# Two PSUM copies per scan step moved from VectorE to ScalarE in a two-layer hybrid trunk

## The chip, the cores and the metric

One core of one Trainium2 chip runs the whole program. The metric is device time in microseconds (us), the median over the runs of the kernel. TensorE is PE in the rows, VectorE DVE, ScalarE ACT, GpSimd POOL, SyncE SP; PEld is TensorE's loading of weights.

## The reference

Two layers, each with three parallel mixers over 128 context tokens and 512 latent tokens, D_MODEL 1024. Mixer C is a bidirectional scan with a delta rule; it is the part that the change touches:

```python
def step(state, inp):
    r_t, w_t, k_t, v_t, a_t, b_t = inp
    sa = jnp.einsum('bhij,bhj->bhi', state, a_t)
    state = (state * w_t[:, :, None, :] + sa[..., None] * b_t[:, :, None, :]
             + v_t[..., None] * k_t[:, :, None, :])
    y_t = jnp.einsum('bhij,bhj->bhi', state, r_t)
    return state, y_t
...
for d, s0 in ((0, s0_f), (1, s0_b)):
    ...
    s_fin, y_d = _wkv_scan(s0.astype(f32), rh, hd(decay), k_d, vh, -kk, kk * hd(a), reverse=(d == 1))
```

Everything else (attention of mixers A and B, gates, projections, norms) stays as it is.

## The kernel before

The program is written tile by tile; a scheduler with its own model of times then puts the instructions of each engine into one fixed order, and each engine runs its list in that order. So an instruction that waits holds back all that stands behind it on its engine. When a line moves to another engine, the scheduler makes the whole order anew.

The tokens of mixer C are cut into ten chunks of 64 (two of context, eight of latent tokens), the eight heads into four pairs. For a pair of heads `prepare` does in turn `c_prep` (decays, keys), `c_pairs` (products inside a chunk, tiles `L1` and `AB`), `c_inverse` and `c_bonus`; then `c_scan` walks the ten chunks, both directions and both heads at once. While the scan of pair p runs, the code draws from a stream (`pump`): the preparation of pair p+1, and projections of 128 columns (tile `pcm`, lines 227 to 229, "fillers" below) whose weights (two buffers) are loaded, rounded on ScalarE (`whi`, line 176) and subtracted on VectorE or GpSimd (`wlo`, line 177).

`c_inverse` (lines 653 to 702) inverts the triangular blocks. Its core is one chain on VectorE: a transpose (line 656), 30 steps of a product (line 662, writes `NF`) and a sum (line 664, writes `LN`), a transpose (line 666), two copies (line 673, with two of ScalarE at line 671) and a last transpose (line 674). Then TensorE has two rounds of small 32x32 products, `px` (line 683) and `py` (line 695), with copies between them. There are eight such inversions, four in each layer.

A scan step, of which a scan has ten and the program 80, goes like this:
- line 771: eight products into PSUM tile `sca` from the state half and the value half of `VZ`;
- lines 773 and 774: the first 64 rows of `sca`, one copy for each head, into `Wb` (tile `wbd`), 64x128 elements each;
- line 777: products of `Wb` with `AB` (the inverse) into `scb`;
- lines 779 and 780: `scb`, one copy for each head, into `VZ`;
- line 782: GpSimd copies that into `Ub` (`ubd`); line 786: products for the state from `VZ`; line 790: products from `Ub`, added in `sca`;
- line 803: VectorE updates the state in `VZ` with four instructions; line 808: ScalarE copies the outputs from `sca` into `YY`.

`Wb` and `Ub` have two buffers each, `VZ` one. After the scan `c_gn` normalises (lines 818 to 834, mostly VectorE) and `c_out` transposes and adds (`pyt`, lines 847 to 852) inside the next scan. The last scan of a layer has hardly any projections beside it for its first steps.

Of the kernel before, what the change touches and what calls it, by code (L numbers as in the profile page):

```python
# [107 lines left out]
class Trunk:  # L108
# [595 lines left out]
    def c_scan(self, l, e, ps, rate, prev):  # L704

        nc, V, S, G, PE = self.nc, self.V, self.S, self.G, self.PE
        sm = cs = self.cs
        p, L1, AB, BT, gm, VZ = e.p, e.L1, e.AB, e.BK, e.gm, e.VZ

        def pc(name):  # L710
            return ps.tile([128, 512], F32, tag="c", name=name)

        PR = (slice(0, 64), slice(64, 128))
        QR = (slice(64, 128), slice(0, 64))

        e.YY = YY = cs.tile([128, 20, 64], F32, tag="YY", name="YY")
        step = 0
        for n, base in ((2, 0), (8, 2)):
            ctxp = n == 2
            if ctxp:  # L720
                for h in range(2):
                    G.memset(VZ[h][PR[h], 0:2, :], 0.0)
                Zg = sm.tile([128, 2, 64], F32, tag="Zg", name="Zg", bufs=2)
                G.memset(Zg, 0.0)
            else:
                Z0 = sm.tile([128, 2, 64], F32, tag="Z0", name="Z0")
                nc.sync.dma_start(out=Z0, in_=self.I["zinit"][l, p])
                for h in range(2):
                    r_ = PR[h]
                    S.copy(out=VZ[h][r_, base, :], in_=Z0[r_, 0])  # L730
                    S.mul(out=VZ[h][r_, base + n - 1, :], in_=Z0[r_, 1], mul=gm[r_, 10 + base + n - 1:10 + base + n])

            def pair(cf, cb):

                a, b = base + cf, base + cb
                if a < b:
                    return slice(a, b + 1, b - a)
                return slice(a, b - 1 if b else None, b - a)

            for k in range(n):  # L740
                cf, cb = k, n - 1 - k
                up = pair(cf, cb)
                uu = (base + cf, 10 + base + cb)
                cc = (base + cf, base + cb)
                last = k == n - 1
                need_z = ctxp or not last
                gi = (base + k, None if last else 10 + base + n - 2 - k)
                if need_z and not (ctxp and k == 0):
                    Zg = sm.tile([128, 2, 64], F32, tag="Zg", name="Zg", bufs=2)
                    for h in range(2):  # L750
                        r_ = PR[h]
                        if not last:
                            g2 = gm[r_, gi[0]:gi[1] + 1:gi[1] - gi[0]]
                            G.tensor_tensor(out=Zg[r_], in0=VZ[h][r_, up, :], in1=g2.unsqueeze(2).to_broadcast([64, 2, 64]),
                                            op=ALU.mult)
                        else:
                            G.tensor_scalar(out=Zg[r_, 0], in0=VZ[h][r_, cc[0], :], scalar1=gm[r_, gi[0]:gi[0] + 1],
                                            scalar2=None, op0=ALU.mult)
                            G.tensor_copy(out=Zg[r_, 1], in_=VZ[h][r_, cc[1], :])
                Wb, Ub = self.wbd[step % 2], self.ubd[step % 2]  # L760
                step += 1
                if step == 5 and prev:
                    self.c_out(prev, ps)
                ca, cb_ = pc("sca"), pc("scb")

                a4 = ca[:, 0:256].rearrange("p (d h i) -> p d h i", d=2, h=2)
                b4 = cb_.rearrange("p (x d h i) -> p x d h i", x=2, d=2, h=2)

                for h in range(2):
                    for d in range(2):  # L770
                        PE.matmul(a4[:, d, h], lhsT=L1[h][:, uu[d]].rearrange("p a s -> p (a s)"), rhs=VZ[h][:, cc[d], :],  # L771
                                  start=(h == 0 and d == 0), stop=False, skip_group_check=True)
                S.copy(out=Wb[PR[0], :, 0], in_=a4[0:64, :, 0])
                V.tensor_copy(out=Wb[PR[1], :, 1], in_=a4[0:64, :, 1])
                self.pump(rate)
                for d in range(2):
                    PE.matmul(cb_[:, d * 128:d * 128 + 128], lhsT=AB[:, uu[d]].rearrange("p a s -> p (a s)"),
                              rhs=Wb[:, d].rearrange("p h i -> p (h i)"), start=True, stop=True, skip_group_check=True)
                S.copy(out=VZ[0][PR[0], up, :], in_=b4[0:64, 0, :, 0])  # L779
                V.tensor_copy(out=VZ[1][PR[1], up, :], in_=b4[0:64, 0, :, 1])  # L780
                for h in range(2):
                    G.tensor_copy(out=Ub[PR[h], :, h], in_=VZ[h][PR[h], up, :])  # L782
                self.pump(rate)
                if need_z:
                    for d in range(2):
                        PE.matmul(cb_[:, 256 + d * 128:384 + d * 128], lhsT=BT[:, uu[d]].rearrange("p h i -> p (h i)"),  # L786
                                  rhs=e.VZt[:, :, cc[d], :], start=True, stop=True, skip_group_check=True)
                self.pump(rate)
                for d in range(2):
                    PE.matmul(ca[:, d * 128:d * 128 + 128], lhsT=AB[:, uu[d]].rearrange("p a s -> p (a s)"),  # L790
                              rhs=Ub[:, d].rearrange("p h i -> p (h i)"), start=False, stop=True, skip_group_check=True)
                if need_z:
                    if last:
                        Zf = sm.tile([128, 2, 64], F32, tag="Zf", name="Zf")
                    for h in range(2):
                        r_ = PR[h]
                        for d in range(2):
                            src = b4[r_, 1, d, h]
                            dst = Zf[r_, d] if last else VZ[h][r_, cc[d] + (1 if d == 0 else -1), :]
                            if gi[d] is None:  # L800
                                V.tensor_tensor(out=dst, in0=src, in1=Zg[r_, d], op=ALU.add)
                            else:
                                V.scalar_tensor_tensor(out=dst, in0=src, scalar=gm[r_, gi[d]:gi[d] + 1], in1=Zg[r_, d],  # L803
                                                       op0=ALU.mult, op1=ALU.add)
                    if last:
                        nc.sync.dma_start(out=self.O["nst"][l, p], in_=Zf)
                for h in range(2):
                    S.copy(out=YY[QR[h], uu[0]:uu[1] + 1:uu[1] - uu[0], :], in_=a4[64:128, :, h])
# [833 lines left out]
```

## Time and profile before

| what | value |
|---|---|
| median of 3 runs | 2282.05 us (2279.15 to 2290.32) |
| the profiled execution | 2288.99 us |
| its span, first to last instruction | 2287.3 us |
| mean granted TensorE clock | 0.947 of 2.4 GHz |
| TensorE busy | 2112.1 us (92%) |
| VectorE busy | 1547.8 us (68%) |
| ScalarE busy | 1155.0 us (50%) |
| GpSimd busy | 528.7 us (23%) |

A row of waits names who waited, for whom, how long in total, how often, and the longest. A clock of 1.00 in a stretch is 2.4 GHz, 0.50 is 1.2 GHz. The scans run from about 114 us to 740 us (layer 0) and from about 1310 us to 1832 us (layer 1).

### The profile page before, as it was taken

How to read it: one execution, taken by the hardware profiler on the slowest of the kernel's cores; microseconds unless marked ns; L12 is line 12 of the kernel's file. 1: busy time of each engine (PE TensorE's matmuls, PEld its weight loads, DVE VectorE, ACT ScalarE, POOL GpSimd, SP SyncE). 2: the span in 40 equal slices, each digit the busy share in tenths (PEclk: the TensorE clock that was granted, in tenths of full speed). 3: DMA queues.
4: the chain of work that ended last, by engine and by line, in shares of the span. 5: the costliest groups of instructions: out<-in, count | busy, mean ns of one | idle time of the engine just before them, and what ended most of it. 6: DMA issues, size and time to landing. Idle time of an engine off the chain costs nothing.

```text
span 2287.3 us, 40446 instructions
## 1 busy us (share of the span) xinstructions
PE 2112.1 (92%) x15380; PEld 2004.8 (88%) x15380; DVE 1547.8 (68%) x3096; ACT 1155.0 (50%) x2574; POOL 528.7 (23%) x680
## 2 busy tenths in 40 slices
PE   8989999999889889999989999998997888899998
PEld 6989999999788768889989999998997876788998
DVE  4666776877845677766647867668576467777673
ACT  4544545554444567762355545545353456677332
POOL 3121324234232221102031022221222222111111
PEclk9998989989899999999999999898897889999999
DMA  6232223222223311036612322232122221111562
GB/s 231 79 96 74 85 78 101 70 89 92 91 87 110 106 38 39 31 101 209 192 53 89 98 75 79 77 101 71 54 94 79 83 88 44 35 47 44 181 194 83
DMA packets 111763, 209.71 MB, mean 92 GB/s; under 512 B 14416, under 2 KB 33488, under 8 KB 111568
## 3 DMA queue, kind: packets, MB, share of 16 engines
q1 hardware_dynamic: 111568, 207.12, 28.3%
q8 instruction: 121, 1.98, 0.4%
q14 instruction: 74, 0.61, 0.1%
HBM read 163.52 MB, written 43.55 MB: 91 GB/s over the span
## 4 chain that ended last, share of the span: by engine, by line
PE 69%; DVE 15%; ACT 8%; issue 4%; DMA 3%; POOL 1%; DVEq 0%; SPq 0%; ACTq 0%; POOLq 0%
PE pcm L227 11%; PE pcm L228 10%; PE pcm L229 10%; PE sc L958 3%; PE pA L612 3%; PE sca L771 2%; PE pm L180 2%; PE pm L182 2%; PE pm L181 2%; PE pp L976 2%; PE scb L786 2%; DVE wlo L177 1%; PE pout L180 1%; PE pout L182 1%; PE pout L181 1%
## 5 line engine op out<-in xcount | busy, mean ns | idle before, releaser
L227 PE MATMUL pcm<-hh,whi 128*128 128x320 f32 x1952 | 630.9, 323 | 21.4 <-DVE modc L254 5.8
L229 PE MATMUL pcm<-hh,wlo 128*128 128x320 f32 x1952 | 621.4, 319 | 7.1 <-DVE wlo L177 7.1
L228 PE MATMUL pcm<-hl,whi 128*128 128x320 f32 x1952 | 620.8, 318 | 0.0
L227 PEld LDWEIGHTS pcm<-hh,whi 128*128 128x128 f32 x1952 | 377.3, 193 | 29.3 <-DVE modc L254 6.8
L229 PEld LDWEIGHTS pcm<-hh,wlo 128*128 128x128 f32 x1952 | 376.3, 193 | 10.4 <-DVE wlo L177 9.4
L228 PEld LDWEIGHTS pcm<-hl,whi 128*128 128x128 f32 x1952 | 377.4, 193 | 1.3
L176 ACT CAST whi<-wraw 128x512 fp32r<-128x512 f32 (+1 forms) x356 | 226.3, 666 | 295.8 <-PE pcm L228 104.1
L177 DVE TENSOR_TENSOR wlo<-wraw,whi 128x512 fp32r<-128x512 f32 (+1 forms) x262 | 208.1, 809 | 84.9 <-ACT whi L176 83.5
L177 POOL TENSOR_TENSOR wlo<-wraw,whi 128x512 fp32r<-128x512 f32 x94 | 123.4, 1328 | 161.4 <-ACT whi L176 126.2
L782 POOL COPY ubd<-VZ 64x128 f32<-64x128 f32 x160 | 62.4, 390 | 406.2 <-ACT VZ L779 345.1
L961 DVE TENSOR_REDUCE nm<-sc 128x1 f32<-128x640 f32 x128 | 104.4, 819 | 27.7 <-PE sc L958 26.3
L166 DVE TENSOR_TENSOR pl<-pp,ph 128x512 fp32r<-128x512 f32 x160 | 107.0, 684 | 22.5 <-ACT ph L165 19.6
L182 PE MATMUL pm<-yh,wlo 128*128 128x320 f32 x384 | 118.9, 310 | 0.3 <-DVE wlo L177 0.3
L180 PE MATMUL pm<-yh,whi 128*128 128x320 f32 x384 | 118.8, 309 | 0.0
L181 PE MATMUL pm<-yl,whi 128*128 128x320 f32 x384 | 118.6, 309 | 0.0
L963 ACT ACTIVATE P<-sc,nm 128x640 f32<-128x640 f32 x128 | 102.0, 798 | 26.7 <-DVE nm L961 22.0
L165 ACT CAST ph<-pp 128x512 fp32r<-128x512 f32 x160 | 91.7, 588 | 37.8 <-PE pp L976 20.3
L976 PE MATMUL pp<-small,P 128*128 128x128 f32 x640 | 98.4, 278 | 2.7 <-ACT RB L1004 2.2
L771 PE MATMUL sca<-VZ,L 128*128 128x64 f32 x640 | 94.6, 286 | 3.0 <-DVE VZ L803 2.2
L771 PEld LDWEIGHTS sca<-VZ,L 128*128 128x128 f32 x640 | 91.2, 208 | 6.0 <-DVE VZ L803 4.0
L976 PEld LDWEIGHTS pp<-small,P 128*128 128x128 f32 x640 | 78.1, 143 | 12.8 <-ACT RB L1004 4.3
L662 DVE TENSOR_TENSOR NF<-LN 128x30 f32<-128x30 f32 (+14 forms) x240 | 84.9, 354 | 6.5
(376 smaller groups left out, 4800.1 us busy)
## 6 DMA issues: line engine op xcount, KB each, us to landing
wraw<-in_win SPq DMA_DIRECT2D x156, 256.0 KB, 3.0
wraw<-in_wg SPq DMA_DIRECT2D x96, 256.0 KB, 3.1
wraw<-in_wmod SPq DMA_DIRECT2D x64, 256.0 KB, 3.0
gsp<-gt SPq DMA_DIRECT2D x48, 320.0 KB, 2.5
gt<-gsp SPq DMA_DIRECT2D x48, 320.0 KB, 3.3
wraw<-in_wo SPq DMA_DIRECT2D x24, 512.0 KB, 4.3
cm<-gsl SPq DMA_DIRECT2D x26, 320.0 KB, 2.6
wraw<-in_wmod SPq DMA_DIRECT2D x16, 512.0 KB, 6.8
```

Of the source, the lines that this page charges most:

```text
L166: self.V.tensor_tensor(out=lo, in0=src, in1=f32(hi), op=ALU.subtract)
L176: self.S.copy(out=hi[part], in_=raw)
L177: sub.tensor_tensor(out=lo[part], in0=raw, in1=f32(hi[part]), op=ALU.subtract)
L180: self.PE.matmul(out, lhsT=lh, rhs=rh, start=first, stop=False)
L181: self.PE.matmul(out, lhsT=lh, rhs=rl, start=False, stop=False)
L182: self.PE.matmul(out, lhsT=ll, rhs=rh, start=False, stop=last)
L227: PE.matmul(p[0:m, 0:H], lhsT=wh[:, kt], rhs=self.hh[:, kt, rs], start=(kt == 0), stop=False)
L228: PE.matmul(p[0:m, 0:H], lhsT=wh[:, kt], rhs=self.hl[:, kt, rs], start=False, stop=False)
L229: PE.matmul(p[0:m, 0:H], lhsT=wl[:, kt], rhs=self.hh[:, kt, rs], start=False, stop=(kt == KT - 1))
L771: PE.matmul(a4[:, d, h], lhsT=L1[h][:, uu[d]].rearrange("p a s -> p (a s)"), rhs=VZ[h][:, cc[d], :], start=(h == 0 and d == 0), stop=False ...
L961: V.tensor_reduce(out=nm, in_=sc[:, :, 0:H], axis=AX.XY, op=ALU.max, negate=True)
L976: PE.transpose(p[:, qt * 128:(qt + 1) * 128], Ps[qt][:, t * 128:(t + 1) * 128], self.ident)
```

## The change

Of the four copies out of PSUM in a scan step two ran on ScalarE (head 0) and two on VectorE (head 1). Now all four run on ScalarE, each in the place of the code where it stood.

```diff
                 S.copy(out=Wb[PR[0], :, 0], in_=a4[0:64, :, 0])
-                V.tensor_copy(out=Wb[PR[1], :, 1], in_=a4[0:64, :, 1])
+                S.copy(out=Wb[PR[1], :, 1], in_=a4[0:64, :, 1])
                 self.pump(rate)
...
                 S.copy(out=VZ[0][PR[0], up, :], in_=b4[0:64, 0, :, 0])
-                V.tensor_copy(out=VZ[1][PR[1], up, :], in_=b4[0:64, 0, :, 1])
+                S.copy(out=VZ[1][PR[1], up, :], in_=b4[0:64, 0, :, 1])
```

The scheduler's order changes with it on all engines. Three places follow.

ScalarE at the 15th of the 80 scan steps, in the second scan of layer 0; before (`gt` is a gate, `TP` and `TM` are decays, `whi` rounded weights):

```order
L773 COPY wbd_561<-sca 64x2x64
L1272 ACTIVATE gt<-pcm 128x320
L527 ACTIVATE TP<-lw 128x10x64
L527 ACTIVATE TM<-lw 128x10x64
L779 COPY VZ<-scb 64x2x64
L176 CAST whi<-wraw 128x512
```

and ScalarE at the same step now:

```order
L773 COPY wbd_561<-sca 64x2x64
L774 COPY wbd_561<-sca 64x2x64
L518 ACTIVATE ta<-pw,dv 128x320 x2
L176 CAST whi<-wraw 128x512 x2
L779 COPY VZ<-scb 64x2x64
L780 COPY VZ<-scb 64x2x64
L1272 ACTIVATE gt<-pcm 128x320
```

The copies of a pair stand next to each other; that holds for all 80 pairs of lines 773 and 774 and for 77 of the 80 of lines 779 and 780. What stands between the pairs has changed.

VectorE at the end of the seventh inversion (the third of layer 1); before:

```order
L664 TENSOR_TENSOR LN<-LN,NF 128x2x29
L774 COPY wbd_12919<-sca 64x2x64
L822 TENSOR_REDUCE mean<-BK 128x10
L662 TENSOR_TENSOR NF<-LN 128x30
L823 TENSOR_SCALAR mean<-mean 128x10
L664 TENSOR_TENSOR LN<-LN,NF 128x30
L824 TENSOR_TENSOR BK<-BK,mean 128x640
L666 STREAM_TRANSPOSE NF<-LN 128x1024
L828 TENSOR_REDUCE var<-BK 128x10
L673 COPY AB<-NF 32x20x32 x2
L237 TENSOR_SCALAR gs<-var 128x10
L674 STREAM_TRANSPOSE NF<-LN 128x1024
```

and VectorE at the end of the same inversion now:

```order
L824 TENSOR_TENSOR BK<-BK,mean 128x640
L662 TENSOR_TENSOR NF<-LN 128x58
L664 TENSOR_TENSOR LN<-LN,NF 128x2x29
L662 TENSOR_TENSOR NF<-LN 128x30
L664 TENSOR_TENSOR LN<-LN,NF 128x30
L828 TENSOR_REDUCE var<-BK 128x10
L666 STREAM_TRANSPOSE NF<-LN 128x1024
L177 TENSOR_TENSOR wlo<-wraw,whi 128x512
L237 TENSOR_SCALAR gs<-var 128x10
L177 TENSOR_TENSOR wlo<-wraw,whi 128x512
L673 COPY AB<-NF 32x20x32 x2
L674 STREAM_TRANSPOSE NF<-LN 128x1024
```

The copy of line 774 is gone from the chain, the rows of `c_gn` (822 to 828) stand earlier in it, and two subtractions of weights stand ahead of line 673.

TensorE at the third inversion (layer 0), from `px` on; before (`pbn` is the bonus of mixer C):

```order
L683 MATMUL px<-NF,AB 32x32 x40
L771 MATMUL sca<-VZ,L_3528 128x64
L695 MATMUL py<-AB,LN 32x32 x40
L571 MATMUL pbn<-prh,bones 128x320
L572 MATMUL pbn<-prl,bones 128x320
L777 MATMUL scb<-wbd_561,AB 128x128
```

and TensorE from the same `px` on now:

```order
L683 MATMUL px<-NF,AB 32x32 x40
L229 MATMUL pcm<-hh,wlo 128x320
L227 MATMUL pcm<-hh,whi 128x320
L228 MATMUL pcm<-hl,whi 128x320
L229 MATMUL pcm<-hh,wlo 128x320
L227 MATMUL pcm<-hh,whi 128x320
```

Now 25 products of projections stand between `px` and `py` there, and 20 behind `py`; before there were none. At the fourth, seventh and eighth inversion there are none before and none now.

## Rows read from the trace of the kernel before

**Rows 1.** The page's first part: busy time (share of the span) and instructions.

```profile
PE 2112.1 (92%) x15380; PEld 2004.8 (88%) x15380; DVE 1547.8 (68%) x3096; ACT 1155.0 (50%) x2574; POOL 528.7 (23%) x680
```

**Rows 2.** The four copies, grouped by line: busy us, mean ns | idle before.

```profile
L780 DVE COPY VZ<-scb 64x128 f32<-64x128 f32 x80 | 22.7, 284 | 45.5 <-ACT VZ L779 44.0
L774 DVE COPY wbd<-sca 64x128 f32<-64x128 f32 x80 | 22.7, 284 | 39.3 <-ACT wbd L773 37.5
...
L773 ACT COPY wbd<-sca 64x128 f32<-64x128 f32 x80 | 20.6, 257 | 47.1 <-PE sca L771 46.4
L779 ACT COPY VZ<-scb 64x128 f32<-64x128 f32 x80 | 20.5, 256 | 49.9 <-PE scb L777 49.3
```

**Rows 3.** Timeline, a bare step: start, length, engine, line [idle before <-releaser].

```profile
1763.73 0.53 ACT L808 COPY YY<-sca 64x128 f32<-64x128 f32 x2 [0.85 <-PE sca L790]
...
1764.88 0.26 ACT L773 COPY wbd<-sca 64x128 f32<-64x128 f32 x1 [0.62 <-PE sca L771]
1765.17 0.28 DVE L774 COPY wbd<-sca 64x128 f32<-64x128 f32 x1 [0.89 <-ACT wbd L773]
...
1765.51 0.71 PE L777 MATMUL scb<-wbd,AB 128*128 128x128 f32 x4 [0.72 <-DVE wbd L774]
1766.31 0.26 ACT L779 COPY VZ<-scb 64x128 f32<-64x128 f32 x1 [1.18 <-PE scb L777]
...
1766.67 0.28 DVE L780 COPY VZ<-scb 64x128 f32<-64x128 f32 x1 [1.22 <-ACT VZ L779]
...
1767.01 0.71 PE L786 MATMUL scb<-VZ,BK 128*128 128x128 f32 x4 [0.79 <-DVE VZ L780]
```

**Rows 4.** TensorE's waits over the span: us in total, times, longest us.

```profile
PE px L683 <- DVE NF L674: 19.8, 4, 9.8
PE scb L777 <- DVE wbd L774: 16.5, 15, 2.6
...
PE scb L786 <- DVE VZ L780: 10.1, 12, 2.2
PE pcm L229 <- DVE wlo L177: 7.1, 9, 2.7
```

**Rows 5.** Timeline, two copies of VectorE that came late.

```profile
1586.92 0.26 ACT L773 COPY wbd<-sca 64x128 f32<-64x128 f32 x1
...
1589.13 0.28 DVE L774 COPY wbd<-sca 64x128 f32<-64x128 f32 x1
...
1589.47 1.22 PE L777 MATMUL scb<-wbd,AB 128*128 128x128 f32 x4 [2.59 <-DVE wbd L774]
...
1776.91 0.26 ACT L779 COPY VZ<-scb 64x128 f32<-64x128 f32 x1 [1.18 <-PE scb L777]
...
1778.69 0.28 DVE L780 COPY VZ<-scb 64x128 f32<-64x128 f32 x1
...
1779.03 1.22 PE L786 MATMUL scb<-VZ,BK 128*128 128x128 f32 x4 [2.21 <-DVE VZ L780]
```

**Rows 6.** VectorE's copies by line, 1443 to 1604.5 us, then 1555 to 1605 us.

```profile
L774 DVE COPY wbd<-sca 64x128 f32<-64x128 f32 x13 | 3.7, 283 | 5.9 <-ACT wbd L773 5.6
L780 DVE COPY VZ<-scb 64x128 f32<-64x128 f32 x12 | 3.4, 284 | 11.1 <-ACT VZ L779 10.9
...
L774 DVE COPY wbd<-sca 64x128 f32<-64x128 f32 x4 | 1.1, 282 | 0.1
...
L780 DVE COPY VZ<-scb 64x128 f32<-64x128 f32 x3 | 0.9, 284 | 0.5 <-ACT VZ L779 0.4
```

**Rows 7.** Stretches: length, busy PE, PEld, DVE, ACT, POOL, clock, DMA share, GB/s.

```profile
200.00:210.00 10.00, 9.92 (x114) 9.49 (x114) 1.73 (x4) 2.96 (x7) 0.24 (x1) 0.73 0.01 2
...
480.00:490.00 10.00, 10.00 (x131) 9.75 (x129) 7.34 (x14) 5.33 (x14) 2.58 (x4) 0.50 0.28 89
...
1600.00:1610.00 10.00, 5.46 (x116) 5.46 (x117) 6.69 (x9) 3.78 (x5) 1.98 (x1) 0.50 0.02 4
1610.00:1620.00 10.00, 10.00 (x81) 9.94 (x80) 6.18 (x17) 3.48 (x8) 3.66 (x6) 0.50 0.14 49
```

## The prediction

> **What bounds the kernel now.** I read the busy times first, then TensorE's waits, then the timeline of the scan steps, and last the clock by stretches. TensorE is busy for 92% of the span, VectorE for 68%, ScalarE for 50% [rows 1]. So time is won only where TensorE stands idle or runs at the lower clock. Of its waits three touch this change: 19.8 us in four waits for the end of the inverse (line 674 on VectorE), 16.5 us in 15 waits for line 774 and 10.1 us in 12 waits for line 780, the two copies that are moved [rows 4]. In the timeline of a step with no filler beside it the pair of copies is already serial: VectorE's copy starts at 1765.17, just as ScalarE's copy of 1764.88 has ended, and TensorE starts at 1765.51 [rows 3]. And where VectorE is full, its copy comes late: ScalarE is done at 1587.18, VectorE's copy starts at 1589.13, and TensorE idles 2.59 us; at 1778.69 the same happens behind the rows of `c_out`, for 2.21 us [rows 5]. After the inversions the clock is at 0.50, which is 1.2 GHz, in whole stretches of 10 us [rows 7].
>
> **The change part by part.** It moves 160 copies of 284 ns from VectorE, 45.4 us of work, and adds 160 of 257 ns on ScalarE, 41 us [rows 2]. VectorE's share falls from 68 to 66%, ScalarE's rises from 50 to 52%; no DMA moves.
>
> *(a) The bare step.* From ScalarE's start to TensorE's start the first pair takes 1765.51 - 1764.88 = 0.63 us, the second 1767.01 - 1766.31 = 0.70 us [rows 3]. With both on ScalarE the pair is 0.53 us (the two copies of line 808 stand back to back in that time) and then a release of TensorE, which I take to be VectorE's: 1765.51 - 1765.45 = 0.06. That is 0.59, so 0.04 and 0.11 us less, 0.15 for a step. About seven steps in each layer's last scan are bare: 14 x 0.15 = 2.1 us. In the other 66 steps fillers mostly hide this; if they hid nothing it would be 80 x 0.15 = 12. I take 2, the bare steps alone, since TensorE is busy elsewhere.
>
> The Trainium skill ("ScalarE: Activation LUTs", What ACT_TABLE_LOAD costs) says that back-to-back instructions of ScalarE overlap by about 93 ns. The rows of line 808 do not show it: two took 0.53 where one copy takes 0.26 [rows 3]. By the page a pair would be an estimated 0.42 us and the bare steps would give 14 x 0.22 = 3 us more.
>
> *(b) Copies that came late on VectorE.* The 27 waits for lines 774 and 780 add up to 26.6 us [rows 4]. A wait of a bare step is 0.72 or 0.79 us [rows 3], and that much stays, since ScalarE needs its 0.53. At 0.7 each 27 x 0.7 = 19 us remain, 7.7 us go. The two of rows 5 alone give 2.59 + 2.21 - 2 x 0.7 = 3.4. Less what (a) has counted I take 6. On ScalarE a copy could be late too, behind a decay or a rounding; but line 773 has stood in that queue all along, and the second copy follows it directly in 157 of 160 pairs. So the bounds are 0 and 7.7.
>
> *(c) The end of the inverse.* VectorE's list between two inversions holds its chain and the scan's copies. From the sixth to the seventh (1443 to 1604.5 us) 25 copies took 7.1 us, and VectorE stood idle 17.0 us ahead of them with everything behind held up [rows 6]. In the last 50 us, which is about the chain itself, there were 7 copies, 2.0 us, and next to no idle time. TensorE then waits for the chain in four of the eight inversions, 9.8 us at most and 19.8 us together [rows 4]. The floor is what the chain loses: 2.0 us in each of the three longer waits, and the rest of the shortest, some 6. The ceiling is all 19.8, since a period frees up to 7.1 + 17.0 = 24 us of VectorE. But the chain cannot start before its inputs, and the new order puts other rows into it (two subtractions of weights ahead of line 673 in the seventh inversion). I take 12, near the middle, as part of the 17 us idle lies ahead of work that the chain waits for. What is late next at those places is the fillers: they have run out, and the small products `px` and `py` must run.
>
> *(d) The clock.* After the seventh inversion, with TensorE idle before it (5.46 of 10 us busy), the clock stays at 0.50 in 1600 to 1620 us; after the third, with no idle time but only small products and no filler between, it is 0.50 in 480 to 490; after the first, which has 22 fillers between `px` and `py`, 0.73 in 200 to 210 [rows 7]. The new order has 25 fillers in the third. At 0.73 instead of 0.50 these 10 us alone give 2.3 us of full clock, the stretch beside it a like amount. A shorter idle time at the seventh should raise the clock sooner, for perhaps as much again. I take 5; the bounds are 0 and 10, the 10 us lost in 20 us at half clock at the seventh.
>
> *(e) ScalarE's longer list.* 160 x 0.257 = 41 us more stand in front of the roundings of weights (line 176), which feed `wlo` and the fillers. TensorE now waits 7.1 us for `wlo` [rows 4]. ScalarE has half of its time free, and the weights are two buffers ahead; this hides it. If that cover were gone, the price is up to 41 us; a third on the path is 14. I take 3 us lost, bounds 0 and 14. GpSimd's copy of line 782 waits for line 780 and gets its input sooner; it is not on the path, so nothing is counted.
>
> The sum: 2 + 6 + 12 + 5 - 3 = 22 us less. The profiled execution took 2288.99 us (span 2287.3 and 1.7 around it), 6.9 us over the median of the runs, 2282.05; it would become 2267. Against the median that is **2260 us**, 1.0% faster. Less than 0.5%, 11 us, can hardly be told from no change here; the three runs alone spread over 11 us.
>
> **The rivals.**
>
> *VectorE's free time is filled again.* The scheduler has moved rows of `c_gn` and subtractions of weights to earlier places of the chain. Then only the floor of (c) comes: 2 + 0 + 6 + 0 - 3 = 5 us, 2277 us. For it speaks the order at the seventh inversion; against it, that the total of VectorE's work falls by 45 us and all the work moved was due anyway.
>
> *Only the step changes.* The pair was serial before and is serial now; if VectorE's chain was held not by the copies but by its inputs, just the bare steps gain: 2280 us. For it speaks the copies' small share of the last 50 us [rows 6]; against it the late copies of rows 5, which were held by VectorE's own queue.
>
> *ScalarE becomes the one waited for (slower).* ScalarE runs its list in order. A pair waits for `sca` or `scb`, and a rounding of weights behind it is late by two copies; `wlo` and then TensorE follow. Price: 41 us on ScalarE. Two thirds on the path, 27 us, less the 8 of (a) and the floor of (c) make 2301 us. It decides from about half on (20 us against 8, 2294), which in the waits means that TensorE's for `wlo` rise from 7 to over 27 us. Against it: ScalarE idles 47.1 and 49.9 us ahead of just these copies, waiting for TensorE [rows 2].
>
> [...]
>
> **How the numbers follow.** Forecast (2260): 0.60. Filled again (2277): 0.22. Only the step (2280): 0.07. ScalarE (2301): 0.11. Faster by over 0.5% is the forecast with a small part of the second, 0.62; within 0.5% 0.27; slower 0.11. The largest gain by the bounds is 12 + 7.7 + 19.8 + 10 = 49 us, 2233; the parts will hardly all be at their end, so I set the low end to 2238. The smallest is 2 + 0 + 6 + 0 - 14, a loss of 6: 2288. From 2238 to 2288 leaves out the slower rival and little else.
>
> **What would show it.** In the changed profile: (a) pairs of 0.53 us on ScalarE and TensorE starting 0.59 after the first; (b) waits for lines 773 to 780 in all near 19 us, with none of over 1 us behind VectorE; (c) waits of `px` for line 674 of some 8 us in place of 19.8; (d) a clock of 0.7 or more after the third inversion and a shorter half-clock stretch at the seventh; (e) waits for `wlo` near 10. I am wrong if `px` waits as long as before, if the half-clock stretches come back elsewhere, or if TensorE's waits for ScalarE's roundings or `wlo` grow by more than 15 us.

## The result, and the profile after

| | before | after |
|---|---|---|
| median | 2281.77 us | **2252.19 us** (2244.64 to 2256.74) |
| ratio, 95% interval | | 0.9861 [0.9823, 0.9898] |
| the profiled execution, its span | 2288.99, 2287.3 us | 2256.74, 2254.7 us |
| TensorE idle (span less busy) | 175.2 us | 153.1 us |
| TensorE busy, the same 15380 instructions | 2112.1 us | 2101.6 us |

The change saves 1.4%, 29.6 us by the medians and 32.3 us between the two profiled executions: 22.1 us of idle time and 10.5 us of busy time, less 0.3 around the span. The forecast was 2260.

The page's first part of the changed kernel [rows 1 of before]; 160 instructions went from VectorE to ScalarE:

```profile
PE 2101.6 (93%) x15380; PEld 1992.5 (88%) x15380; DVE 1506.8 (67%) x2936; ACT 1200.6 (53%) x2734; POOL 527.8 (23%) x680
```

The four copies grouped by line (busy us, mean ns | idle before them); compare [rows 2]:

```profile
L774 ACT COPY wbd<-sca 64x128 f32<-64x128 f32 x80 | 20.6, 258 | 1.1
L780 ACT COPY VZ<-scb 64x128 f32<-64x128 f32 x80 | 20.6, 258 | 1.9
...
L773 ACT COPY wbd<-sca 64x128 f32<-64x128 f32 x80 | 20.6, 257 | 42.3 <-PE sca L771 41.8
```

The moved copies cost what the others cost, and ScalarE has next to no idle time ahead of them: they follow their partners at once. TensorE's waits (total us, times, longest), first of the changed kernel [rows 4]:

```profile
PE px L683 <- DVE NF L674: 15.3, 5, 8.2
...
PE scb L786 <- ACT VZ L780: 6.9, 9, 1.5
PE scb L777 <- ACT wbd L774: 6.8, 10, 1.3
...
PE pcm L229 <- DVE wlo L177: 6.5, 8, 1.8
```

and one more row of the kernel before, which has no counterpart after (GpSimd's copy of line 782 into `ubd`):

```profile
PE sca L790 <- POOL ubd L782: 4.0, 3, 3.1
```

The waits for the copies fell from 26.6 to 13.7 us, those for `ubd` from 4.0 to none, those of `px` from 19.8 to 15.3, those for `wlo` from 7.1 to 6.5: 22.0 us together, about what the idle time fell by. But the waits do not tell how it came. The larger fact shows only in the length of a scan step.

**The steps got shorter.** "Mixed steps" are from here on steps 3 to 10 of the first three scans of each layer, those with fillers beside them: 7 intervals in 6 scans, 42 in all. These are two rows of the windows view for tile `pcm` alone (length, busy PE (number of fillers), clock, DMA share, GB/s): the second scan of layer 0 from its third to its tenth step, and the sum over all six such stretches. First before:

```profile
366.20:468.62 102.42, 74.14 (x444) 1.00 0.31 100
...
sum 625.26, PE 425.26; mean PE 70.88
```

and after:

```profile
353.38:438.23 84.85, 56.90 (x321) 1.00 0.29 96
...
sum 552.46, PE 378.80; mean PE 63.13
```

At a clock of 1.00 in both, this stretch of seven intervals is 17.6 us shorter and holds 123 fillers less. A mixed step takes 625.26 / 42 = 14.89 us before and 552.46 / 42 = 13.15 us after. What the change took out of it is lateness of the pairs of copies. From the start of the first copy to the end of the second, the mean over these steps (3 to 10, so 48 pairs) was 1.63 us (`wbd`) and 1.87 us (`VZ`) before; it is 0.53 and 0.60 now (from the records of lines 773, 774, 779 and 780; the first of [rows 5] is a long one of these). That this lateness is the reason for the long step is what the experiments below test. TensorE hardly waited for it, since fillers stood in its list meanwhile. The same stretches for all instructions, before and after:

```profile
sum 625.26, PE 605.28 PEld 592.25 DVE 484.30 ACT 308.70 POOL 167.66; mean PE 100.88 PEld 98.71 DVE 80.72 ACT 51.45 POOL 27.94
...
sum 552.46, PE 541.05 PEld 528.91 DVE 429.44 ACT 322.10 POOL 168.09; mean PE 90.17 PEld 88.15 DVE 71.57 ACT 53.68 POOL 28.02
```

TensorE stood idle for 20.0 us of them before and for 11.4 after, so waiting on the chip makes only 8.6 of the 72.8 us. The other 64.2 us are busy time. Most of it is fillers, 425.26 - 378.80 = 46.5 us, which the new order has in other places; some is the clock, which was 0.94 and 0.96 in two of the six stretches before and is 1.00 in all now.

**The third and the seventh inversion start sooner.** The end of the seventh inversion, with the steps that lead to it: the last product of the previous pair's `c_out` (line 847), which reads `L1` of that pair, then GpSimd's memset of the same buffer for the next pair (line 500), then the start and the end of the chain (lines 656 and 674). Timeline before:

```profile
1512.31 0.38 PE L847 MATMUL pyt<-small,L 128*128 128x128 f32 x2
1512.81 2.23 POOL L500 MEMSET L<- 64x2560 f32 x1
...
1559.81 1.25 DVE L656 STREAM_TRANSPOSE LN<-NF 128x1024 f32<-128x1024 f32 x1
1602.59 1.90 DVE L674 STREAM_TRANSPOSE NF<-LN 128x1024 f32<-128x1024 f32 x1 [0.27 <-ACT AB L671]
```

and after:

```profile
1489.22 0.27 PE L847 MATMUL pyt<-small,L 128*128 128x128 f32 x1
1490.55 2.23 POOL L500 MEMSET L<- 64x2560 f32 x1
...
1538.46 1.25 DVE L656 STREAM_TRANSPOSE LN<-NF 128x1024 f32<-128x1024 f32 x1 [1.30 <-ACT NF L653]
1580.36 2.08 DVE L674 STREAM_TRANSPOSE NF<-LN 128x1024 f32<-128x1024 f32 x1
```

The sixth inversion ended at 1443.0 before and at 1438.9 after. From there the memset comes after 69.8 us before and 51.6 after; the chain starts after 116.8 and 99.5; it ends after 161.5 and 143.5. So the seventh inversion is done 18 us sooner, but its chain itself is hardly shorter: 1604.49 - 1559.81 = 44.7 us, now 1582.44 - 1538.46 = 44.0. The chain of the third starts 113.1 us after the end of the second before and 96.7 after; those of the fourth (93.5 and 98.8) and the eighth (95.0 and 92.7) move less.

### The profile page after: what moved, and what is told of

The parts are those of the page before. It is cut to its first block, busy times and chain, and to the rows that moved or that the text cites. A ratio compares the mean times of both kernels' runs of the same rounds, so it can differ in the third digit from the quotient of the medians.

```text
span 2254.7 us, 40396 instructions
## 1 busy us (share of the span) xinstructions
PE 2101.6 (93%) x15380; PEld 1992.5 (88%) x15380; DVE 1506.8 (67%) x2936; ACT 1200.6 (53%) x2734; POOL 527.8 (23%) x680
## 4 chain that ended last, share of the span: by engine, by line
PE 68%; DVE 15%; ACT 9%; issue 4%; DMA 3%; POOL 1%; DVEq 0%; SPq 0%; ACTq 0%; POOLq 0%
PE pcm L227 10%; PE pcm L229 10%; PE pcm L228 10%; PE sc L958 3%; PE pA L612 3%; PE sca L771 2%; PE pm L180 2%; PE pm L181 2%; PE pm L182 2%; PE pp L976 2%; PE pout L180 1%; PE pout L182 1%; PE pout L181 1%; PE px L683 1%; ACT whi L176 1%
## 5 line engine op out<-in xcount | busy, mean ns | idle before, releaser
L181 PE MATMUL pm<-yl,whi 128*128 128x320 f32 x384 | 118.7, 309 | 0.0
L803 DVE SCALAR_TENSOR_TENSOR VZ<-scb,gm,Zg 64x64 f32<-64x64 f32 x256 | 62.1, 280 | 45.2 <-PE scb L786 32.6
L612 PE MATMUL pA<-L,BK 128*128 128x128 f32 x640 | 86.6, 278 | 5.8 <-ACT AB L617 5.0
```

The source lines that it names most:

```text
L181: self.PE.matmul(out, lhsT=lh, rhs=rl, start=False, stop=False)
L612: PE.matmul(pA[:, j * 128:(j + 1) * 128], lhsT=BK[:, u].rearrange("p a s -> p (a s)"), rhs=L1[h][:, u].rearrange("p a s -> p (a s)"), star ...
```

## The experiments

At first two theories stood: that VectorE's list held the inversion (Theory 1, the prediction's), and that a new order by the scheduler alone moves the time (Theory 2).

**Half the change, and other orders.** `wbd_only` moves line 774 alone, `vz_only` line 780 alone. `before_swapped` and `after_swapped` write the copy of head 1 ahead of that of head 0, with the engines unchanged:

```diff
-                S.copy(out=Wb[PR[0], :, 0], in_=a4[0:64, :, 0])
                 S.copy(out=Wb[PR[1], :, 1], in_=a4[0:64, :, 1])
+                S.copy(out=Wb[PR[0], :, 0], in_=a4[0:64, :, 0])
```

> Only the copy of line 774 (into Wb) is on ScalarE; line 780 stays on VectorE. Theory 1 (VectorE's queue: its time and the late copies): about half of the 30 us, 2262 to 2272 us, with TensorE's waits at line 777 near 7 us and those at line 786 still near 10. Theory 2 (the gain is a chance of the order that the scheduler makes anew): anything between 2245 and 2290, not tied to the waits of the copies.

> Only the copy of line 780 (into VZ) is on ScalarE; line 774 stays on VectorE. Theory 1: the other half, 2262 to 2272 us, waits at line 786 near 7 us, those at line 777 still near 16; the two halves together make up the whole within 10 us. Theory 2: anything between 2245 and 2290, and the halves do not add up.

> The kernel before with VectorE's copy written ahead of ScalarE's in both pairs: each engine has the same work, the scheduler makes a new order. Theory 1: 2277 to 2292 us, a little slower if ScalarE's copy now waits for a late one of VectorE. Theory 2: it moves by as much as the change did, 15 us or more, in either direction.

> The changed kernel with head 1 copied ahead of head 0: same work on the same engines, new order. Theory 1: 2245 to 2260 us, like the changed kernel. Theory 2: it moves by 15 us or more, for example back towards 2270 to 2285.

Each ratio from here on is to executions of the kernel before that ran beside that kernel (medians 2281.55 to 2285.51 us); differences in us are taken from the medians 2281.77 and 2252.19.

Measured: 2258.15 (ratio to before 0.9879 [0.9854, 0.9904]), 2247.96 (0.983 [0.981, 0.985]), 2288.8 (1.0022 [1.0003, 1.004]) and 2241.85 us (0.9803 [0.9784, 0.9822]). Either half brings about as much as the whole, so the parts do not add. Another order with the same engines moves 7 and 10 us in the two cases tried, too little for 30, but enough that 10 us between two kernels here say little. Neither theory holds as it stood. What the two halves share with the change is the start of the seventh chain: 100.6 and 98.7 us after the sixth inversion's end (in `before_swapped` 118.7). That led to a third theory. `before_swapped` also shows how the lateness must be measured. Its pairs take only 0.84 and 0.74 us, yet its steps 14.75: VectorE's copy, late as ever, now comes first, and the pair starts late. Counted from the end of the products to the end of the second copy, the two pairs together take 4.5 us of a step in the kernel before and in `before_swapped`, 3.5 and 3.7 in `wbd_only` and `vz_only`, 2.3 in the changed kernel and 2.4 in `after_swapped` (means of the same 48 steps); the length of the step goes with that.

**What starts the inversion (the gate).** `c_out` of the previous pair is written ahead of the scan's fifth step. It reads `L1` of a buffer that the next pair's preparation needs. A slow scan makes it late, and the next inversion with it. `before_cout3` takes the kernel before and writes `c_out` into step 3; `after_cout7` takes the changed kernel and writes it into step 7.

```diff
-                if step == 5 and prev:
+                if step == 3 and prev:
```

> The kernel before, with c_out of the previous pair written into step 3 of the scan in place of step 5 (the same work, two steps sooner; the scheduler makes the order anew). Gate theory: in the mixed stretches the next inversion cannot start before c_out of the previous pair has freed that pair's buffers, so c_out about 25 us sooner does what the four copies did. Expected: the chain of the seventh inversion (line 656) starts at most 102 us after the end of the sixth (before 116.8, after 99.5), the seventh period is 140 to 150 us (before 160.2), the whole 2250 to 2266 us. Rival (VectorE's own list holds c_prep, c_out only stands beside it): line 656 stays at 112 or more, the whole 2275 to 2290.

> The changed kernel, with c_out of the previous pair written into step 7 of the scan in place of step 5. Gate theory: c_out comes some 25 us later (about 70 us after the end of the sixth inversion in place of 45.5), line 656 of the seventh inversion starts at 115 to 128 us in place of 99.5, the seventh period is 160 us or more, and the gain is lost: 2275 to 2300 us. Rival (VectorE's own list): line 656 stays below 106, the whole 2245 to 2262.

Measured: 2276.1 (0.9968 [0.9949, 0.9987]) and 2310.23 us (1.0118 [1.0093, 1.0144]). The place is right in both directions: the chain of the seventh inversion starts 99.7 and 122.7 us after the end of the sixth. `after_cout7` came out 10 us beyond its range (2275 to 2300). In `before_cout3` the memset is released by `c_out` in plain sight, and the inversion is done at 1587.4; but the scan ahead of it then ends only at 1614.2 (timeline; line 808 is the scan's last output, line 773 the first copy of the next scan):

```profile
1496.53 2.23 POOL L500 MEMSET L<- 64x2560 f32 x1 [3.89 <-PE pyt L847]
...
1585.46 1.98 DVE L674 STREAM_TRANSPOSE NF<-LN 128x1024 f32<-128x1024 f32 x1 [0.28 <-ACT AB L671]
1613.64 0.53 ACT L808 COPY YY<-sca 64x128 f32<-64x128 f32 x2 [1.91 <-PE sca L790]
1614.48 0.26 ACT L773 COPY wbd<-sca 64x128 f32<-64x128 f32 x1 [0.31 <-PE sca L771]
```

So the total of `before_cout3` missed its expectation (2250 to 2266): the inversion is no longer late, but the scan with its steps of 15.2 us is, and the next scan starts no sooner than before: its first product from the inverse (line 777) is at 1617.9, 1612.8 in the kernel before. Two chains run beside each other; one alone sped up gives little.

**VectorE's load, or its place in the chain.** `all_vector` has all four copies on VectorE. `dummy_vector` is the changed kernel with 160 copies more on VectorE, for which no product waits; `load_scalar` gives ScalarE four extra copies behind each pair in the first three scans of a layer, for which no product waits either; `delay_scalar` puts four into the chain there:

```diff
                 S.copy(out=Wb[PR[1], :, 1], in_=a4[0:64, :, 1])
+                if p < 3:
+                    for _ in range(4):
+                        S.copy(out=Wb[PR[1], :, 1], in_=a4[0:64, :, 1])
```

> The kernel before, with all four copies of a step on VectorE: the dose in the other direction. VectorE's busy time rises by some 45 us to about 1593, ScalarE's falls to about 1114. Both theories: slower or no gain. If VectorE's late copies lengthen the steps, TensorE's waits for lines 773 to 780 rise to 40 us or more (26.6 before) and the whole to 2292 to 2315. If the four copies matter only by the handover between two engines in the bare step, the pair gets shorter here too (one engine, one release) and the whole is 2275 to 2285.

> The changed kernel with VectorE's 160 copies put back as extra work that nothing waits for: it copies the same halves of Wb and VZ from SBUF into a scratch tile. VectorE's busy time is back near 1540 us; no product of TensorE waits for these copies. If the gain is VectorE's free time (its list moves faster), it goes: 2270 to 2285. If the gain is that the steps no longer wait for VectorE's turn, it stays: 2245 to 2262, waits for lines 773 to 780 near 14 us, seventh period below 150 us.

> The changed kernel, with a delay put into the chain of a step in the first three scans of each layer: ScalarE makes the copy of head 1 five times in a row into the same place, so a pair takes some 0.53 + 4 x 0.26 = 1.6 us, as long as it took before on average in those steps (1.63 and 1.87 us). VectorE stays relieved of all its copies (its busy time stays near 1507 us), and the nearly bare last scan of each layer is left as it is in the changed kernel. Theory of the step's chain (the gain is that the pair no longer takes 1.6 to 1.9 us in the mixed steps): the steps 3 to 10 are back near 15 us (14.9 before, 13.2 after), line 656 of the seventh inversion at 110 us or more after the end of the sixth, the whole 2270 to 2292 us. Rival (VectorE's free time): steps and seventh period as in the changed kernel, the whole 2248 to 2262 us.

> The changed kernel with the same extra work for ScalarE in the same scans (four copies of 64x128 behind each pair, 123 us in all), but into a scratch tile: no product waits for it, so it is load beside the chain, not delay in it. Theory of the step's chain: most of the gain stays, 2250 to 2266 us, pairs of 0.53 to 0.6 us, TensorE's waits for wlo below 15 us. If ScalarE's longer list is what costs (term e of the prediction), waits for wlo and for ScalarE's products rise by over 15 us and the whole to 2270 or more.

Measured: 2275.72 (0.997 [0.9955, 0.9986]), 2262.77 (0.9921 [0.9893, 0.995]), 2338.16 (1.0241 [1.0205, 1.0277]) and 2264.11 us (0.9924 [0.9898, 0.9949]).

`dummy_vector` has VectorE as busy as before, but out of the chain:

```profile
PE 2099.7 (93%) x15380; PEld 1994.4 (88%) x15380; DVE 1550.2 (69%) x3096; ACT 1200.0 (53%) x2734; POOL 525.6 (23%) x680
```

19 of the 29.6 us stay (0.8 us above the range for that theory), and the steps take 13.4 us. In `all_vector` the pairs are short (0.64 and 0.61 us) but start late: 1.69 and 1.33 us after the product's end, against 0.50 for both before, since now the first copy too stands in VectorE's list. The steps stay at 14.8 us, and only 6 us are won; VectorE's 40 us more cost nothing that can be seen. The first expectation missed (waits for the copies 25.7 us and not 40, no loss). The total lies in the range of the second, but the handover is not what shortens the steps, since they stay long. `delay_scalar` loses everything with VectorE relieved: its sum over the 42 mixed steps, in the view shown above, is

```profile
sum 649.70, PE 395.92; mean PE 65.99
```

15.5 us for a step, and the seventh chain starts 132.5 us after the sixth inversion. It went past its expectation, since the pairs came out at 2.91 and 2.30 us and not at 1.6: the scheduler set other ScalarE work between the copies. So it shows that a delay in this chain costs time without VectorE; it does not price a microsecond of it. As many copies beside the chain (142 us of ScalarE by their rows) cost 12 us. The page's first part and the wait for `wlo` of `load_scalar`:

```profile
PE 2102.1 (92%) x15380; PEld 1994.3 (88%) x15380; DVE 1498.1 (66%) x2936; ACT 1344.7 (59%) x3214; POOL 525.1 (23%) x680
...
PE pcm L229 <- DVE wlo L177: 4.5, 7, 1.5
```

**Both chains together.** `after_swapped_cout3` and `after_cout3` write `c_out` into step 3 with all four copies on ScalarE, with and without the swap.

> The changed kernel with head 1 copied ahead of head 0 (2241.85 us) and with c_out in step 3 of the scan in place of step 5. If c_out still holds the next inversion back when the steps are short, the periods of the third, fourth, seventh and eighth inversions get shorter by up to 10 us each, and fillers are left over for the last scan: 2220 to 2240 us. If scans and inversions are by now balanced, as the small gain of that edit on the kernel before (0.3%) says, 2238 to 2262 us.

> The changed kernel with c_out in step 3 of the scan in place of step 5 and nothing else: the fourth corner beside the kernel before (2282), the changed kernel (2252) and c_out in step 3 of the kernel before (2276). If the two edits simply add, 2252 - 6 = 2246 us. If they need each other (short steps let the scan keep up with the earlier inversion, the earlier c_out lets the inversion keep up with the shorter scan), 2218 to 2232 us with a seventh period near 126 us.

Measured: 2218.74 (0.972 [0.9689, 0.9751]) and **2218.12 us** (0.9696 [0.967, 0.9722]), 3% below the kernel before and 1.5% below the changed one. The two edits need each other: -6 and -30 us alone, -64 together. The swap's 10 us are gone here. In `after_cout3` the seventh inversion ends at 1537.2 and the scan ahead of it at 1556.3, where it was 1614.2 with the long steps:

```profile
1446.44 2.23 POOL L500 MEMSET L<- 64x2560 f32 x1 [7.08 <-PE pyt L847]
1495.64 1.25 DVE L656 STREAM_TRANSPOSE LN<-NF 128x1024 f32<-128x1024 f32 x1
...
1535.13 2.05 DVE L674 STREAM_TRANSPOSE NF<-LN 128x1024 f32<-128x1024 f32 x1
...
1555.79 0.53 ACT L808 COPY YY<-sca 64x128 f32<-64x128 f32 x2
```

Its waits of `px`, and the busy times (the wait was 19.8 us before, 15.3 after):

```profile
PE 2080.8 (94%) x15380; PEld 1975.8 (89%) x15380; DVE 1510.4 (68%) x2936; ACT 1197.5 (54%) x2734; POOL 532.1 (24%) x680
...
PE px L683 <- DVE NF L674: 3.0, 3, 1.3
```

All kernels side by side. A step is the mean of the 42 mixed steps by the starts of the first copy of the `wbd` pair; the last three columns are us from the end of the sixth inversion to the memset that follows `c_out`, to the start and to the end of the seventh inversion's chain:

| kernel | median us | step us | memset | chain starts | ends |
|---|---|---|---|---|---|
| before | 2281.77 | 14.89 | 69.8 | 116.8 | 161.5 |
| after | 2252.19 | 13.15 | 51.6 | 99.5 | 143.5 |
| wbd_only | 2258.15 | 13.63 | 55.8 | 100.6 | 146.5 |
| vz_only | 2247.96 | 13.88 | 51.5 | 98.7 | 144.6 |
| before_swapped | 2288.80 | 14.75 | 68.7 | 118.7 | 161.6 |
| after_swapped | 2241.85 | 13.01 | 50.9 | 97.8 | 142.0 |
| before_cout3 | 2276.10 | 15.19 | 52.4 | 99.7 | 143.3 |
| after_cout7 | 2310.23 | 13.06 | 73.9 | 122.7 | 161.9 |
| all_vector | 2275.72 | 14.75 | 64.5 | 112.2 | 158.3 |
| dummy_vector | 2262.77 | 13.38 | 52.4 | 101.6 | 148.6 |
| load_scalar | 2264.11 | 13.18 | 55.7 | 99.2 | 145.4 |
| delay_scalar | 2338.16 | 15.47 | 86.0 | 132.5 | 173.0 |
| after_swapped_cout3 | 2218.74 | 13.16 | 34.9 | 84.2 | 125.7 |
| after_cout3 | 2218.12 | 13.15 | 34.2 | 83.4 | 124.9 |

From the memset to the start of the chain it is 43.5 to 50.0 us in all fourteen, from 34 to 86 us of memset time. That is the gate. Kernels with both a short step and an early memset are fast; one of the two is not enough (`before_cout3`, `after_cout7`).

## Why the prediction was right in sum, and where it was wrong

It named 2260 and the measurement is 2252, inside the range; the sum of 22 us against 32.3 in the profiled execution is made of terms that are off in both directions. That it came so close is in part luck: 7.5 us too much in (c) cancel half of the 14.4 us that (a) with (b), (d) and a term set at nothing had too little.

**(a) The bare step: right.** A step of the last scan of layer 1, after:

```profile
1738.49 0.26 ACT L773 COPY wbd<-sca 64x128 f32<-64x128 f32 x1 [0.69 <-PE sca L771]
1738.77 0.26 ACT L774 COPY wbd<-sca 64x128 f32<-64x128 f32 x1
1739.08 0.71 PE L777 MATMUL scb<-wbd,AB 128*128 128x128 f32 x4 [0.69 <-ACT wbd L774]
1739.89 0.26 ACT L779 COPY VZ<-scb 64x128 f32<-64x128 f32 x1 [0.86 <-PE scb L777]
1740.17 0.26 ACT L780 COPY VZ<-scb 64x128 f32<-64x128 f32 x1
1740.48 0.71 PE L786 MATMUL scb<-VZ,BK 128*128 128x128 f32 x4 [0.69 <-ACT VZ L780]
```

TensorE starts 1739.08 - 1738.49 = 0.59 us after the first copy, and 0.59 after the second pair's; 0.63 and 0.70 before [rows 3]. That is the 0.59 of the prediction. Its count of bare steps was too high: before, the last scans have no filler in 4 steps of layer 0 and in 6 of layer 1, so 10 and not 14 steps, 1.5 us. The copies start 0.28 us apart and take 0.26 each: the overlap that the Trainium skill states for back-to-back ACTIVATEs ("ScalarE: Activation LUTs", What ACT_TABLE_LOAD costs) is not there for these copies. It is there elsewhere in the same trace: of the 195 ACTIVATEs that directly follow another (less than 60 ns behind its end), 100 overlap it by 93 ns or more. A copy of line 773 can overlap an ACTIVATE ahead of it, too, here by 1492.05 + 0.94 - 1492.87 = 0.12 us:

```profile
1492.05 0.94 ACT L518 ACTIVATE ta<-pw,dv 128x320 f32<-128x320 f32 x2
1492.87 0.25 ACT L773 COPY wbd<-sca 64x128 f32<-64x128 f32 x1
```

Why the pairs of the step have none is not shown.

**(b) The late copies: the place right, the size wrong twice.** 12.9 us of waits went, with (a), where 2 + 6 = 8 were summed and 2 + 7.7 was the bound. The bound kept 0.7 us for each of 27 waits; only 19 are left. That is the small error. The large one is the view. The lateness was counted where TensorE idled for it; it amounted to 1.10 + 1.27 = 2.4 us in each mixed step (1.63 to 0.53 and 1.87 to 0.60), nearly all under fillers. "Since TensorE is busy elsewhere", as term (a) put it for the steps with fillers, was the step that failed, here as there: the scan is a chain of its own, and the order that the scheduler made around the late copies gave it longer steps.

**(c) The end of the inverse: a gain, but not where the sum put it, and not by its reason.** The waits of `px` fell by 4.5 us and not by 12, less than the floor of 6. The floor said that the chain loses the 2.0 us of copies inside it; it lost 0.7 (44.7 to 44.0), for the scheduler set rows of `c_gn` and subtractions of weights there, as the rival "filled again" had it. What moved is the start of the chain, 17 us, by a path that the prediction had in one half sentence ("the chain cannot start before its inputs") and did not follow: scan step, `c_out`, `L1`, preparation. Two kernels show that VectorE's freed time is not the main reason. `dummy_vector` takes it back, and 19 us of the gain stay. `after_cout7` has VectorE as free as the changed kernel, yet TensorE's idle time is back above that of before (2302.9 - 2095.7 = 207 us), and TensorE waits 72.2 us for the end of the inverse:

```profile
PE 2095.7 (91%) x15380; PEld 1990.5 (86%) x15380; DVE 1500.8 (65%) x2936; ACT 1198.3 (52%) x2734; POOL 530.8 (23%) x680
...
PE px L683 <- DVE NF L674: 72.2, 7, 23.9
```

**(d) The clock: right in direction, too small.** TensorE's busy time fell by 10.5 us for the same instructions, with a mean granted clock of 0.955 in place of 0.947; 5 were taken, 10 was the bound. Ten-us stretches after (length, busy PE, PEld, DVE, ACT, POOL, clock, DMA share, GB/s), at the third, the fourth and the seventh inversion; compare [rows 7]:

```profile
470.00:480.00 10.00, 10.00 (x163) 9.74 (x159) 2.45 (x5) 1.88 (x4) 0.00 (x0) 0.83 0.37 119
480.00:490.00 10.00, 9.22 (x72) 8.99 (x69) 4.35 (x13) 4.89 (x11) 5.58 (x6) 1.00 0.27 93
...
600.00:610.00 10.00, 2.23 (x15) 1.75 (x14) 9.38 (x19) 4.75 (x6) 4.62 (x4) 0.76 0.27 97
610.00:620.00 10.00, 8.29 (x163) 8.23 (x164) 4.30 (x6) 2.19 (x5) 0.00 (x0) 0.50 0.02 5
...
1580.00:1590.00 10.00, 9.96 (x182) 9.60 (x181) 7.10 (x10) 3.63 (x8) 0.55 (x1) 0.91 0.31 93
1590.00:1600.00 10.00, 10.00 (x48) 10.00 (x48) 5.12 (x14) 4.05 (x10) 4.66 (x8) 0.58 0.16 49
```

With fillers between `px` and `py` and no idle time ahead, the third inversion keeps 0.83 and then 1.00 (0.50 before); at the seventh one stretch at 0.58 is left of two at 0.50. At the fourth, where the fillers still run out (2.23 of 10 us busy), it falls to 0.50.

**(e) ScalarE's longer list: within its bounds.** Waits for `wlo` went from 7.1 to 6.5 us. `load_scalar` put 142 us on ScalarE and cost 12 us, a twelfth; by that share the 41 us of the change cost 3.4, against the 3 taken. The ordering noise of up to 10 us leaves room on either side. The waits for `ubd` were set at nothing, as "not on the path": GpSimd's copy gets its input sooner, and 4.0 us of TensorE's waits went.

**The rivals.** "Filled again" was right about the chain's inside and wrong about the sum. "Only the step" falls with (b) as a sum; but its premise, that VectorE's chain was held by its inputs, is what the runs show. What it missed is that shorter steps bring those inputs sooner. "ScalarE" as the one waited for did not come; `load_scalar` carries 142 us on top of that load and stays 0.8% below the kernel before.

**What stays open.** How many fillers stand in a step is fixed by the scheduler's order, which is made from its own model of times; the chip then runs that order. Of the 1.74 us of a step 0.2 us is idle time of TensorE and the rest mostly fillers that stand elsewhere, so most of the gain in the step is the scheduler's reply to the move and not a wait that the chip was spared. No kernel had the new engines in the old order, so what the move would bring without a new order is not shown. That `after_swapped` is 10 us faster than the changed kernel is not explained beyond the spread of orders. Nor is it that `dummy_vector` is 10.6 us slower: a part of that size of the gain may still be VectorE's freed time, since no second order of `dummy_vector` was run.

## What to carry to other kernels

A copy that comes late under cover of other work is not free when it stands in a serial chain: measure the chain (a step's length, and a pair from the end of what it reads to the end of its last copy), not only the bound engine's waits. Where two chains wait for each other, follow back what starts each one, buffers that are to be freed among it, and speed up both: here -6 and -30 us apart became -64 together. And where a scheduler makes the order, run the same edit in another order before a difference of 0.5% is believed.

## What was not expected of the hardware

One duration: a copy of the same shape on ScalarE takes longer from SBUF than from PSUM. The groups of `load_scalar` on ScalarE, the extra copies and the pair's own (busy us, mean ns | idle before):

```profile
L778 ACT COPY dum<-wbd 64x128 f32<-64x128 f32 x240 | 70.9, 296 | 6.7
L787 ACT COPY dum<-VZ 64x128 f32<-64x128 f32 x240 | 70.9, 295 | 6.8
L775 ACT COPY wbd<-sca 64x128 f32<-64x128 f32 x80 | 20.6, 258 | 1.1
```

295 ns from SBUF against 258 from PSUM, so the extra load came out at 142 us where 123 were reckoned. The copies' 257 ns and the releases of the bare step were as the rows of before had them.
